# Strassen products of a decoder trunk: a second set of raw weight buffers, another order for each stage's first products, and later sums for two hidden pairs

## The chip, the cores and the metric

The kernel runs on one core of a Trainium2 chip. The metric is the device time of one execution in microseconds (us). Engine names as in the profile: PE (TensorE matmuls), PEld (its weight loads), DVE (VectorE), ACT (ScalarE), POOL (GpSimd), SP (SyncE, which here issues nearly all DMAs).

## The reference

A decoder trunk over 1024 positions with a width of 1024 and two layers, all in float32. Layer 0 mixes tokens with a chunked spatial gate, layer 1 with dilated window attention (three groups of eight heads, head width 64). After each mixer comes a dense MLP:

```python
for layer in range(DEPTH):
    y = _rms_norm(h, mix_norm_g[layer])
    ...
    h = h + y
    y = _rms_norm(h, mlp_norm_g[layer])
    h = h + jnp.square(jax.nn.relu(y @ w_up[layer])) @ w_down[layer]
return _rms_norm(h, final_norm_g)
```

`w_up` is 1024 x 4096 and `w_down` 4096 x 1024, so the two MLPs and the attention's 1024 x 4608 `w_qkv` are most of the work.

## The kernel before, in words

Everything is kept transposed: the stream `h` is eight tiles of 128 rows by 1024 positions. Each float32 operand is split into a high part (rounded by ScalarE, L203) and the rest (a VectorE subtraction, L204), and each block of 128 x 128 by 512 takes three matmuls (`three`, L359).

*Seven products.* The up projection, the down projection and the attention's q, k, v products work on 2 x 2 blocks by a Strassen scheme of seven products instead of eight (`product`, L364): the outputs c11, c12, c21, c22 of a pair of output tiles come from products 1 to 7 and a few sums. A product is 12 matmuls of 512 columns in the up projection, which has 16 pairs q = 0 to 15 in each layer. The order of the products is written out by hand: 5, 6, 1, 7, 3, 2, 4 in `mlp` (L690) and `Down.run` (L819), and 6, 1, 5, 7, 2, 3, 4 in `seven` (L1076, attention). Some products go into the bank of an earlier one, to be added there (3 on 5's, 2 on 1's, 4 on 7's); such a product has to wait until the earlier content is read. There are eight PSUM banks: three of a pool for `mm_bank`, five for `at_bank`.

*Weights.* `Weights` (L370) loads four raw blocks of a pair (`raw`, L161, four buffers in all), forms the combinations on POOL (L389 to L394) and splits each of the seven (tile `wp`; eight buffers). `ahead` does a step of the next pair's weights after each product of this one: 4, then 1, then 5, 6, 7, 3, 2. A raw buffer is free when its split has read it; the next load into it waits for that on SP's queue, and what stands behind on SP waits too.

*Inputs.* `Terms` (L424) makes the input combinations t1 to t7 of a stage while its first output tiles (q = 0 and 1 in the up projection, four tiles in the attention) are computed in the plain, classical way, since these need no combinations. The first half of the positions is s = 0, the second s = 1. After that come the pairs in seven products, from q = 2 on.

*Hidden pairs.* The up projection's outputs go through a squared ReLU on ScalarE (L673, L674). The down projection, whose inner index is the 15 first hidden pairs, needs seven combinations of each (`hidden_terms`, L676: four VectorE sums), which are stored to DRAM and loaded again (`Down.inputs`, L814). The down projection goes through 18 groups t; a full group has four hidden pairs (28 input tiles) and products of 12 matmuls; the first and last groups are smaller.

*Buffers.* `slot` gives one of 38 slots of 4 KB a partition for `h`, the inputs' split pairs and more; `temp` one of 11 of 2 KB (tag t), `spare` one of 2 (tag b).

*Order.* PE's instructions keep the order of the program. On the other engines a scheduler places them when the program is built, by its own estimate of readiness and by the place in the program; `tc.high_priority(offset=PRIO)` moves an instruction up by 60 places. Small side tasks of the attention (scores, transposes, values) are put between the products by `Flow`, which counts PE's time in ns and starts a task when its time has come; `LAT` holds these delays.

Of the kernel before, what the change touches and what calls it, by code (L numbers as in the profile page):

```python
# [10 lines left out]
F32 = mybir.dt.float32  # L11
# [6 lines left out]
P = 128  # L18
# [94 lines left out]
def trunk(ctx: ExitStack, tc: tile.TileContext, xT, w_u, w_v, w_o, w_s, b_s, w_qkv, w_bo, rel,  # L113
# [255 lines left out]

    class Weights:  # L370


        def __init__(self, src, own=None, place=None):
            self.own, self.place = own or raw, place or wpair
            self.w = {}
            self.r = {ij: load(src(*ij), self.own()) for ij in ((1, 0), (1, 1), (0, 0), (0, 1))}
# [7 lines left out]
        def steps(self):  # L384
# [11 lines left out]
            for p, src in ((5, r[1, 0]), (6, r[1, 1]), (7, r3), (3, r[0, 0]), (2, r[0, 1])):  # L396
                self.split(p, src)
                yield

# [289 lines left out]

    def mlp(layer, x, first, last):  # L690


        def up_weights(q):
            return Weights(up(layer, q))
# [4 lines left out]
        for s in range(2):  # L699
# [4 lines left out]
            for b, (q, i) in zip(banks, tiles):  # L704
# [3 lines left out]
                if s and i:  # L708
                    hidden_terms(q, c[q, 0, 0], c[q, 1, 0], c[q, 0, 1], c[q, 1, 1], c[q, 0, 0])
# [6 lines left out]
        for q in range(2, 16):  # L716
# [4 lines left out]
            d = at_bank()  # L721
            product(d, w[5], x.t[5])
            more()
            c22 = temp()
            nc.scalar.activation(c22, d, AF.Copy)  # L725
            if down:
                down.take(14, held, SEVEN[:4])
            b = at_bank()
            product(b, w[6], x.t[6])
            more()  # L730
            if down:
                down.take(14, held, SEVEN[4:])
            a = mm_bank()
            product(a, w[1], x.t[1])
            more()
            u = temp()
            with tc.high_priority(offset=PRIO):
                nc.scalar.activation(u, a, AF.Copy)  # L738
                nc.vector.tensor_tensor(u, u, b, op=ALU.add)
            if down:  # L740
                down.early(SEVEN[:4])
            e = at_bank()
            product(e, w[7], x.t[7])
            more()
            with tc.high_priority(offset=PRIO):
                nc.vector.tensor_tensor(c22, c22, e, op=ALU.add)  # L746
            nc.vector.tensor_tensor(c22, c22, u, op=ALU.add)
            squared(c22)
            if down:
                down.early(SEVEN[4:])  # L750
            product(d, w[3], x.t[3], True)
            more()
            c12 = temp()
# [788 lines left out]
```

## Time and profile before

| what | value |
|---|---|
| runs of the kernel before | 2202.07 us median of 3 (2201.95 to 2205.04) |
| the profiled execution: time | 2201.35 us |
| its span, first to last instruction | 2199.6 us |
| mean granted TensorE clock | 0.987 |
| VectorE busy, share of the span | 1664.0 us, 76% |
| ScalarE busy | 1132.7 us, 51% |
| POOL busy | 608.3 us, 28% |
| mean DMA rate | 110 GB/s |

In the rows of the order of time, the columns are the start in us, the length in us, engine, line, operation, the tile written and the tiles read, shapes, and the number of instructions merged; in brackets stands the idle time of the engine before, and what ended it. `SPq` is SP's queue, where the DMAs are issued.

### The profile page before, as it was taken

How to read it: one execution, taken by the hardware profiler on the slowest of the kernel's cores; microseconds unless marked ns; L12 is line 12 of the kernel's file. 1: busy time of each engine (PE TensorE's matmuls, PEld its weight loads, DVE VectorE, ACT ScalarE, POOL GpSimd, SP SyncE). 2: the span in 40 equal slices, each digit the busy share in tenths (PEclk: the TensorE clock that was granted, in tenths of full speed). 3: DMA queues.
4: the chain of work that ended last, by engine and by line, in shares of the span. 5: the costliest groups of instructions: out<-in, count | busy, mean ns of one | idle time of the engine just before them, and what ended most of it. 6: DMA issues, size and time to landing. Idle time of an engine off the chain costs nothing.

```text
span 2199.6 us, 30242 instructions
## 1 busy us (share of the span) xinstructions
PE 2129.9 (97%) x10242; PEld 1758.3 (80%) x10242; DVE 1664.0 (76%) x2984; ACT 1132.7 (51%) x2294; POOL 608.3 (28%) x442
## 2 busy tenths in 40 slices
PE   7999999999999999998999999999989999999998
PEld 5888886888877888786888788887878888778887
DVE  6875259777788887788787877877887767888866
ACT  6744235555565444346665666664455556544433
POOL 1100114333323332443212222201333332332345
PEclk9999999999999999998999999999999999999999
DMA  6321113444444443321112111141044443554432
GB/s 221 100 83 48 48 41 112 157 151 151 151 163 162 158 157 120 110 82 45 45 42 46 42 53 42 46 161 47 29 168 153 154 148 128 175 166 152 151 110 77
DMA packets 155935, 241.81 MB, mean 110 GB/s; under 512 B 33161, under 2 KB 47620, under 8 KB 155780
## 3 DMA queue, kind: packets, MB, share of 16 engines
q1 hardware_dynamic: 154880, 238.65, 33.3%
q8 instruction: 80, 1.31, 0.3%
q10 hardware_dynamic: 900, 1.23, 0.2%
q14 instruction: 75, 0.61, 0.1%
HBM read 176.21 MB, written 63.61 MB: 109 GB/s over the span
## 4 chain that ended last, share of the span: by engine, by line
PE 76%; DVE 12%; issue 3%; ACT 3%; DMA 3%; POOL 1%; SPq 0%; DVEq 0%; POOLq 0%; ACTq 0%
PE mm L180 37%; PE at L180 37%; DVE wp L204 2%; DVE t L204 2%; PE at L187 2%; DMA r<-in_w_dn 1%; DVE y L204 1%; DMA t<-hid 1%; ACT t L1143 1%; ACT wp L203 1%; DVE h L833 1%; DVE q L1062 1%; DVE k L1062 1%; DVE tr L204 1%; DVE hx L204 1%
## 5 line engine op out<-in xcount | busy, mean ns | idle before, releaser
L203 ACT ACTIVATE wp<-r 128x512 fp32r<-128x512 f32 (+3 forms) x492 | 295.2, 604 | 352.2 <-PE at L180 165.1
L204 DVE TENSOR_TENSOR wp<-r,wp 128x512 fp32r<-128x512 f32 (+3 forms) x492 | 385.5, 787 | 76.2 <-ACT wp L203 73.6
L180 PE MATMUL at<-hx,wp 128*128 128x512 f32 x1770 | 414.4, 390 | 5.5 <-DVE h L833 2.8
L180 PE MATMUL mm<-y,wp 128*128 128x512 f32 x1608 | 404.6, 398 | 1.3 <-ACT t L738 0.8
L180 PEld LDWEIGHTS at<-hx,wp 128*128 128x128 f32 x1770 | 331.9, 188 | 77.0 <-DVE h L833 3.4
L389 POOL TENSOR_TENSOR t<-r 128x512 f32<-128x512 f32 (+3 forms) x78 | 110.3, 1414 | 907.3 <-DMA r<-in_w_up 281.5
L180 PEld LDWEIGHTS mm<-y,wp 128*128 128x128 f32 x1608 | 302.9, 191 | 68.2 <-ACT t L738 1.7
L180 PE MATMUL at<-t,wp 128*128 128x512 f32 x1344 | 318.7, 393 | 8.2 <-DVE t L746 8.2
L180 PEld LDWEIGHTS at<-t,wp 128*128 128x128 f32 x1344 | 255.2, 190 | 62.6 <-DVE t L746 9.0
L180 PE MATMUL mm<-t,wp 128*128 128x512 f32 x768 | 192.5, 397 | 2.3 <-DVE t L204 2.1
L180 PE MATMUL mm<-hx,wp 128*128 128x512 f32 x708 | 172.2, 390 | 5.6 <-DVE b L859 5.6
L261 POOL TENSOR_TENSOR t<-t 128x512 f32<-128x512 f32 (+1 forms) x54 | 69.1, 1279 | 385.4 <-ACT t L252 383.5
L204 DVE TENSOR_TENSOR hx<-t,hx 128x512 fp32r<-128x512 f32 x192 | 164.1, 870 | 11.7 <-ACT hx L203 11.6
L180 PEld LDWEIGHTS mm<-t,wp 128*128 128x128 f32 x768 | 141.5, 189 | 33.0 <-DVE t L204 2.5
L180 PEld LDWEIGHTS mm<-hx,wp 128*128 128x128 f32 x708 | 132.4, 188 | 34.9 <-ACT wp L203 5.0
L180 PE MATMUL mm<-y,whi 128*128 128x512 f32 x512 | 158.3, 390 | 0.0
L203 ACT ACTIVATE hx<-t 128x512 fp32r<-128x512 f32 x192 | 117.9, 627 | 52.5 <-DMA t<-hid 47.8
L180 PE MATMUL at<-y,wp 128*128 128x512 f32 x552 | 138.5, 392 | 3.0 <-ACT t L725 3.0
L833 DVE TENSOR_TENSOR h<-h,at 128x512 f32<-128x512 f32 x144 | 98.1, 683 | 51.6 <-PE at L180 50.5
L394 POOL TENSOR_TENSOR r<-r 128x512 f32<-128x512 f32 (+3 forms) x78 | 106.6, 1366 | 94.2 <-issue 77.3
L391 POOL TENSOR_TENSOR r<-r 128x512 f32<-128x512 f32 (+3 forms) x78 | 118.3, 1516 | 47.4 <-DVE wp L204 43.7
L180 PEld LDWEIGHTS at<-y,wp 128*128 128x128 f32 x552 | 103.7, 189 | 26.6 <-ACT t L725 3.8
(212 smaller groups left out, 3270.8 us busy)
## 6 DMA issues: line engine op xcount, KB each, us to landing
t<-hid SPq DMA_DIRECT2D x182, 256.0 KB, 4.6
hid<-t SPq DMA_DIRECT2D x140, 256.0 KB, 2.3
r<-in_w_up SPq DMA_DIRECT2D x128, 256.0 KB, 2.7
r<-in_w_dn SPq DMA_DIRECT2D x88, 256.0 KB, 2.6
r<-in_w_qkv SPq DMA_DIRECT2D x72, 256.0 KB, 2.7
hid<-b SPq DMA_DIRECT2D x56, 256.0 KB, 2.2
r<-in_w_v SPq DMA_DIRECT2D x48, 256.0 KB, 3.5
h<-in_xT SPq DMA_DIRECT2D x16, 256.0 KB, 4.3
```

Of the source, the lines that this page charges most:

```text
L180: nc.tensor.matmul(out, lhsT, rhs, **kw)
L187: nc.tensor.transpose(out, src, ident)
L203: nc.scalar.activation(hi, src, AF.Copy)
L204: nc.vector.tensor_tensor(lo, src, hi.bitcast(F32), op=ALU.subtract)
L261: nc.gpsimd.tensor_tensor(self.acc, self.acc, sq, op=ALU.add)
L389: tt(r3, r[0, 0], r[1, 0], op=ALU.subtract)
L391: tt(r[1, 1], r[1, 0], r[0, 0], op=ALU.subtract)
L394: tt(r[0, 0], r[0, 1], r[1, 1], op=ALU.subtract)
L833: engine.tensor_tensor(hs[i, s], hs[i, s], src, op=ALU.add)
L1062: nc.vector.scalar_tensor_tensor(lo, a, sc, hi.bitcast(F32), op0=ALU.mult, op1=ALU.subtract)
L1143: nc.scalar.activation(p[:, c], p[:, c], AF.Exp, bias=m, scale=-1.0, accum_out=dn)
```

## The change

1. Weights of the up projection from q = 4 on and of the down projection's groups t = 1 to 16 take only two of their four raw blocks from the four raw buffers; the other two share one slot (`mixed`). So two pairs' raw blocks can be there at once.
2. The first pair in seven products of each up projection (q = 2) and of the attention runs in the order 1, 3, 6, 2, 7, 5, 4, with more banks, and its weights are split in the order 4, 1, 3, 6, 2, 7, 5. The copy of the first product and all sums that read banks are placed 60 places up.
3. The other pairs of the up projection go 6, 1, 5, 7, 2, 3, 4, and the default order of the weights' splits becomes 4, 1, 2, 5, 6, 7, 3 (the down projection's order of products stays).
4. The squares of the classical pairs q = 0 and 1 are stored as they are; their four sums are made at the end of q = 5 and q = 8 from four reloaded tiles (`classical_terms`).
5. The transposes of the first attention unit's values come 5000 ns later in `Flow`.

```diff
+    def mixed():
+        got = []
+        def one():
+            if not got:
+                two = slot((P, 2, HALF), F32, "r2")
+                got.extend([raw(), two[:, 1, :], raw(), two[:, 0, :]])
+            return got.pop()
+        return one
...
-            for p, src in ((5, r[1, 0]), (6, r[1, 1]), (7, r3), (3, r[0, 0]), (2, r[0, 1])):
-                self.split(p, src)
+            src = {2: r[0, 1], 5: r[1, 0], 6: r[1, 1], 7: r3, 3: r[0, 0]}
+            for p in self.late:
+                self.split(p, src[p])
                 yield
+    FIRST = (3, 6, 2, 7, 5)
...
+    def classical_terms(q):
+        c11, c12, c22, c21 = (load(hidden_tile(q, what), temp()) for what in (1, (0, 1), 3, 2))
+        t3, t4 = spare(), spare()
+        tt = nc.vector.tensor_tensor
+        tt(t3, c22, c12, op=ALU.subtract)
+        tt(c12, c12, c11, op=ALU.subtract)
+        tt(c11, c22, c12, op=ALU.subtract)
+        tt(t4, c21, c11, op=ALU.subtract)
+        kept(q, {7: t3, 5: c12, 6: c11, 4: t4})
...
-            return Weights(up(layer, q))
+            return Weights(up(layer, q), own=mixed() if q > 3 else None, **(dict(late=FIRST) if q == 2 else {}))
...
-                if s and i:
-                    hidden_terms(q, c[q, 0, 0], c[q, 1, 0], c[q, 0, 1], c[q, 1, 1], c[q, 0, 0])
+                what = {(0, 0): 1, (1, 0): 2, (0, 1): (0, 1), (1, 1): 3}[i, s]
+                kept(q, {what: c[q, i, s]})
...
+            if q == 2:
+                a = mm_bank()
+                product(a, w[1], x.t[1])
+                more()
+                u = first_sum(a)
+                d = at_bank()
+                product(d, w[3], x.t[3])
+                more()
+                b = at_bank()
+                product(b, w[6], x.t[6])
+                more()
+                plus(u, b, u)
+                product(a, w[2], x.t[2], True)
+                more()
+                c11 = temp()
+                squared(c11, a)
+                e = at_bank()
+                product(e, w[7], x.t[7])
+                more()
+                c22 = plus(u, e)
+                f = at_bank()
+                product(f, w[5], x.t[5])
+                more()
+                plus(c22, f, c22)
+                c12 = plus(u, f)
+                plus(c12, d, c12)
+                squared(c12)
+                squared(c22)
+            else:
...
             product(e, w[4], x.t[4], True)
             more()
+            c21 = plus(u, e)
             squared(c21)
+            if q in (5, 8):
+                classical_terms((q - 5) // 3)
...
-                    wn = self.weights(t + 1, **(dict(own=temp, place=pair) if t == 16 else {}))
+                    wn = self.weights(t + 1, **(dict(own=temp, place=pair) if t == 16 else dict(own=mixed())))
...
-            flow.add(v_side(i, t, part), LAT["ve"] + (500 if b is None else 1500))
+            flow.add(v_side(i, t, part), LAT["ve"] + (500 if b is None else 1500) + (5000 if i == 0 else 0))
...
+        if first:
+            a = one(1)
+            u = copied(a)
+            d = one(3)
+            plus(u, one(6), u)
+            one(2, a)
+            put_out(0, 0, a)
+            e = one(7)
+            c22 = plus(u, e)
+            f = one(5)
+            put_out(1, 1, c22, f, True)
+            put_out(0, 1, plus(u, f), d, True)
+        else:
...
-            w = Weights(qkv(*quads[0]))
+            w = Weights(qkv(*quads[0]), late=FIRST)
```

`first_sum` and `copied` are a ScalarE copy of a bank, `plus` a VectorE sum, all under `tc.high_priority(offset=PRIO)`; `one(p)` in `seven` runs product p in a new `mm_bank`, or adds it to the bank that it is given.

156 lines of the change are left out of this document (78 added, 78 removed).

## Prediction

> **What bounds the kernel now.** I read the page first, then the list of what TensorE waited for, and then the order of time around the longest of those waits.
>
> ```profile
> span 2199.6 us, 30242 instructions
> PE 2129.9 (97%) x10242; PEld 1758.3 (80%) x10242; DVE 1664.0 (76%) x2984; ACT 1132.7 (51%) x2294; POOL 608.3 (28%) x442
> PE at L180 <- DVE t L746: 8.2, 2, 4.1
> PE mm L180 <- DVE b L859: 6.5, 4, 2.2
> PE at L187 <- ACT t L1019: 4.5, 1, 4.5
> PE at L180 <- DVE h L833: 3.5, 4, 1.3
> PE at L180 <- ACT t L725: 3.0, 2, 2.1
> PE at L180 <- ACT hx L203: 2.2, 2, 1.1
> PE mm L180 <- DVE t L204: 2.1, 1, 2.1
> ```
>
> TensorE (PE) is busy for 2129.9 of 2199.6 us, and the change leaves its matmuls as they are. So only the remaining 70 us can be won, and what a slowed TensorE clock costs. The columns of the waits are total us, times, longest. L725, L738 and L746 belong to the first pair of seven products of each up projection (each once a layer; L738 shows below); L859, L833 and hx to the down projection; L1019 and the 2.1 of t L204 to the start of the attention products. Here is that first pair, in layer 0 and then in layer 1 (start, length, instructions, idle time before):
>
> ```profile
> 355.47 5.60 PE L180 MATMUL at<-t,wp 128*128 128x512 f32 x24
> 367.34 3.01 PE L180 MATMUL at<-y,wp 128*128 128x512 f32 x12 [0.83 <-ACT t L725]
> 370.84 3.01 PE L180 MATMUL mm<-y,wp 128*128 128x512 f32 x12 [0.49 <-ACT t L738]
> 377.95 10.03 PE L180 MATMUL at<-t,wp 128*128 128x512 f32 x36 [4.10 <-DVE t L746]
> 387.82 2.88 PE L180 MATMUL mm<-y,wp 128*128 128x512 f32 x12
> 390.54 2.88 PE L180 MATMUL at<-t,wp 128*128 128x512 f32 x12
> ...
> 1591.37 5.60 PE L180 MATMUL at<-t,wp 128*128 128x512 f32 x24
> 1604.62 3.02 PE L180 MATMUL at<-y,wp 128*128 128x512 f32 x12 [2.12 <-ACT t L725]
> 1615.10 11.20 PE L180 MATMUL at<-t,wp 128*128 128x512 f32 x36 [4.11 <-DVE t L746]
> 1626.14 2.88 PE L180 MATMUL mm<-y,wp 128*128 128x512 f32 x12
> ```
>
> A product is 12 matmuls and takes 390.54 - 387.82 = 2.72 us. The row at 387.82 is product 1 of the next pair (q = 3), nine products after 355.47. Without waits it would start at 355.47 + 9 x 2.72 = 379.95, so layer 0 loses 7.87 us here. Layer 1 should reach it at 1591.37 + 24.48 = 1615.85 and does at 1626.14: 10.29 lost. The idle times do not add up to that, because the clock fell after the long wait (us, PE busy, granted clock, DMA share, GB/s):
>
> ```profile
> 378.00:382.00 4.00, 4.00 (x11) 0.57 0.52 178
> 1614.00:1621.00 7.00, 5.90 (x14) 0.51 0.60 200
> 420.00:439.10 19.10, 19.10 (x86) 15.82 (x85) 13.47 (x17) 10.09 (x17) 6.30 (x5) 1.00 0.46 152
> ```
>
> The 36 matmuls from 377.95 took 387.82 - 377.95 = 9.87 us where three products take 8.16: 1.71 us of clock. The last row is a later pair, with the busy time of PE, PEld, DVE, ACT and POOL: PE has no idle time there, so nothing that speeds a later pair's weights can gain in it.
>
> **The change, part by part.** *First pair, order 1, 3, 6, 2, 7, 5, 4.* Before, product 3 accumulated on product 5's bank, product 2 on product 1's and product 4 on product 7's, and each waited for a read (L725, L738, L746). Now 3, 6, 7 and 5 have banks of their own and only 2 and 4 wait. Product 2 needs ScalarE's copy of product 1. That copy is now raised by 60 places, but so are the squares of the classical tiles, which come earlier in the program, and ScalarE was late:
>
> ```profile
> 363.78 1.16 ACT L674 ACTIVATE t<-t 128x512 f32<-128x512 f32 x2
> ...
> 366.71 0.58 ACT L725 ACTIVATE t<-at 128x512 f32<-128x512 f32 x1
> ...
> 1601.37 1.16 ACT L674 ACTIVATE t<-t 128x512 f32<-128x512 f32 x2
> 1602.41 0.64 ACT L203 ACTIVATE t<-t 128x512 fp32r<-128x512 f32 x1
> 1603.97 0.60 ACT L725 ACTIVATE t<-at 128x512 f32<-128x512 f32 x1
> ```
>
> These are the last squares of each layer, and L725 in each. Right behind them the copy (0.58) ends at 363.78 + 1.16 + 0.58 = 365.5 and at 1603.1. Product 2 is fourth, due at 355.47 + 8.16 = 363.63 and at 1591.37 + 8.16 = 1599.53. So it waits 1.9 and 3.6 us. Bounds: nothing if the copy goes ahead of the squares; 366.71 + 0.58 - 363.63 = 3.7 and 1603.97 + 0.60 - 1599.53 = 5.0 if it stays where L725 stood. I take the middle, as the program's priorities put it there. An idle time of 3.6 us lies between waits of 2.22 (a row below; the 12 matmuls after it took 3.00, full speed) and 4.10 (half clock after it); it is nearer to the second, so I add 1.7 for the clock in layer 1.
>
> [...]
>
> *Product 4.* L746 read the bank late because VectorE (DVE) was behind with sums and splits:
>
> ```profile
> 1603.87 1.76 DVE L204 TENSOR_TENSOR t<-t,t 128x512 fp32r<-128x512 f32 x1
> 1607.25 0.68 DVE L679 TENSOR_TENSOR b<-t 128x512 f32<-128x512 f32 x1
> 1607.85 1.78 DVE L204 TENSOR_TENSOR wp<-r,wp 128x512 fp32r<-128x512 f32 x1
> 370.33 1.60 POOL L391 TENSOR_TENSOR r<-r 128x512 f32<-128x512 f32 x1 [0.69 <-DVE wp L204]
> 1607.47 1.61 POOL L391 TENSOR_TENSOR r<-r 128x512 f32<-128x512 f32 x1 [0.69 <-DVE wp L204]
> ```
>
> The eight sums of the two classical pairs (L679 to L685, 8 x 0.68 = 5.4 us) leave this place. Product 7's bank is now read by one sum, and product 5 (2.72 us) runs in between. I count this wait as gone: 0.
>
> *What is late next* is the second pair, which now begins with product 6. Its weights are ready after POOL's L391, a ScalarE copy (0.64) and a VectorE split (at worst 1.78, beside POOL): 370.33 + 1.60 + 2.42 = 374.4 and 1607.47 + 1.61 + 2.42 = 1611.5. Product 6 is due four products after product 2 has started: 365.5 + 10.88 = 376.4 and 1614.0. The wait of product 2 covers it by 2.0 and 2.5 us. Without that wait product 6 would be due at 374.5 and at 1591.37 + 7 x 2.72 = 1610.4 and would itself wait 1.1 in layer 1.
>
> So the two starts give 7.87 - 1.9 = 6.0 and 10.29 - 3.6 - 1.7 = 5.0: **11.0 us**, with bounds of 6.1 (rival 1) and 17 (7.87 + 10.29 - 1.1).
>
> *The sums made later*, at q = 5 and 8: four loads on SP's queue, four sums and four stores each. VectorE has 13.47 + 4 x 0.68 = 16.2 of 19.10 us to do, so PE hides it: 0. Bare, it would be 2.7 us at each of four places, 11 in all. The loads stand on SP ahead of the weights of q = 7 and 10; the second raw set has those a pair ahead.
>
> *Steady pairs in order 6, 1, 5, 7, 2, 3, 4*: one ScalarE copy less (10.09 of 19.10 busy), each bank is reused two products after it filled, as products 1 and 7's were; 0.
>
> *Second raw set.* In the up projection 0, as said. In the down projection SP is held by it (rows: total, times, longest; then SP's and PE's order of time):
>
> ```profile
> SPq L169 <- DVE wp L204: 192.5, 60, 7.8
> 677.70 7.95 SPq L169 DMA_DIRECT2D r<-in_w_dn  x3
> 685.70 3.27 SPq L169 DMA_DIRECT2D t<-hid  x7
> 697.13 3.00 PE L180 MATMUL mm<-hx,wp 128*128 128x512 f32 x12 [2.22 <-DVE b L859]
> ```
>
> Between 630 and 900 us, SP waits 192.5 us for a weight split to free a raw buffer, and the loads of the hidden inputs queue behind: seven of them from 685.70, right after weights that took 7.95. Their splits then hold VectorE up, and PE waits 2.22 at 697.13. I count one such wait per layer as gone: 2 x 2.2 = **4.4 us**. Bounds: 0, and all of L859, L833 and hx, 6.5 + 3.5 + 2.2 = 12.2.
>
> *Attention's first products* take banks from the pool of three only:
>
> ```profile
> 996.75 2.82 PE L180 MATMUL mm<-t,wp 128*128 128x512 f32 x10
> 1006.97 1.11 PE L187 MATMUL at<-ident,t 128*128 128x128 f32 x4 [4.53 <-ACT t L1019]
> 1005.81 1.11 ACT L1019 ACTIVATE t<-mm 128x512 f32<-128x512 f32 x1
> 1010.29 1.11 DVE L1062 SCALAR_TENSOR_TENSOR q<-mm,q 128x512 fp32r<-128x512 f32 x1
> ```
>
> Two of the three hold classical tiles until L1019 (1006.92) and L1062 (1011.40). Before, product 6 ran and then the transposes waited for L1019. Now product 1 runs, the transposes come later, and product 3 waits for the same L1019, for a bank. At 1006.92 twelve matmuls are done in either case: 0. Bounds: a gain of 2.1 + 4.5 = 6.6 if ScalarE's order changes; a loss of 1011.40 - 1006.92 - 2.72 = 1.8, product 6 waiting for the third bank.
>
> **Sum.** The profiled execution took 2201.35 us (its span is 2199.6); the median of the runs before is 2202.07, 0.03% above. 2201.35 - 11.0 - 4.4 = **2185.9 us**. A measurement of this kernel can tell about 0.2%, 4.4 us, from no change.
>
> **Rivals.** *1. The waits only change owner.* The copy stays where L725 was: layer 0 gains 7.87 - 3.7 - 1.7 = 2.5, layer 1 10.29 - 5.0 - 1.7 = 3.6, attention loses 1.8, the down projection gains nothing: 2201.35 - 4.3 = 2197.0. For it: ScalarE takes its queue in order, and that order was late by a slow VectorE. Against it: the copy's new priority. Chance 0.14, no change.
>
> *2. The second pair takes the wait.* Its splits go 4, 1, 2, 5, 6, so four stand ahead of 6 on VectorE; if all five take 1.78 beside POOL and four sums of 0.68 come between, 11.6 us from 1603.87 (where the classical sums ended and a split of 1.76 began) plus that 1.76 end at 1617.2, against 1614.0 due: 3.2 late, and much the same in layer 0, 6.4 in all: 2192.3. For it: the 1.78 row against 0.68. Against: four slow splits need four POOL sums beside them. Chance 0.14, faster.
>
> [...]
>
> *3. Slots run out, slower.* A raw set now takes a slot of 38. In the down projection 8 hold the stream and 28 the four groups' inputs, so the two that were free for the next inputs hold raw weights. Splits of the inputs then wait for a product to end, their loads keep the temporaries, and SP is blocked again. At 2.2 us (the wait at 697.13) in half of the 20 full groups that is 22 us: 2201.35 - 11.0 + 22 = 2212. It decides from 11.0 / 2.2 = 5 groups on. Against it: an input's slot is freed seven products before its successor is used. Chance 0.12.
>
> *4. Everything gives.* 17 at the starts, 12.2 in the down projection, 6.6 at the attention: 2165.5; half of the surplus, 2176. For it: the waits are real; against it: the banks and ScalarE's order. Chance 0.12.
>
> **How the numbers follow.** The forecast has 0.48, with a range of its own of 2179 to 2192. Faster: 0.48 + 0.14 + 0.12 = 0.74; within 0.2%: 0.14; slower: 0.12. The range 2172 to 2199 leaves out rival 3 and the far end of rival 4.
>
> **What would show it.** Right: no wait for L746's successor; one wait of 2 and one of 3 to 4 us before the fourth product of the first pairs, on the copy of product 1; SP waiting far less than 192.5 us on weight splits; the attention's first gap unchanged in size, now ahead of product 3. Wrong: idle PE in later pairs at q = 5 to 9, or new short waits on hx in every group of the down projection.

## The result, and the profile after

The changed kernel takes 2182.13 us (median of five runs, 2178.83 to 2192.09) against 2204.02 (median of five, 2201.95 to 2207.61): ratio 0.9907, 95% interval 0.9881 to 0.9933, faster by 0.9%. The forecast was 2185.9, range 2172 to 2199. The profiled execution has the time of the median, 2182.13, and its span is 19.2 us shorter than before.

The page of the changed kernel, and its list of what TensorE waited for (total us, times, longest):

```profile
span 2180.4 us, 30158 instructions
...
PE 2121.8 (97%) x10242; PEld 1755.2 (80%) x10242; DVE 1647.1 (76%) x2987; ACT 1126.3 (52%) x2266; POOL 600.9 (28%) x442
```

```profile
PE mm L180 <- ACT t L750: 6.6, 2, 4.3
...
PE mm L180 <- ACT t L1079: 5.6, 1, 5.6
...
PE at L180 <- DVE h L893: 1.6, 2, 0.8
...
PE mm L180 <- DVE b L919: 0.4, 1, 0.4
```

The wait for a VectorE sum ahead of product 4 (8.2 us in all before) is gone from the list; the copy of product 1 (L750) stands in its place with 6.6. L919 and L893, the successors of the down projection's L859 and L833, went from 6.5 and 3.5 to 0.4 and 1.6.

The first pair of both layers in TensorE's order of time:

```profile
357.28 4.24 PE L180 MATMUL mm<-y,wp 128*128 128x512 f32 x18
...
369.31 4.22 PE L180 MATMUL mm<-y,wp 128*128 128x512 f32 x12 [2.35 <-ACT t L750]
373.34 11.59 PE L180 MATMUL at<-t,wp 128*128 128x512 f32 x48
384.76 2.88 PE L180 MATMUL mm<-y,wp 128*128 128x512 f32 x12
...
1579.01 4.24 PE L180 MATMUL mm<-y,wp 128*128 128x512 f32 x18
...
1592.97 4.51 PE L180 MATMUL mm<-y,wp 128*128 128x512 f32 x12 [4.28 <-ACT t L750]
1597.32 11.04 PE L180 MATMUL at<-t,wp 128*128 128x512 f32 x48
1608.20 2.88 PE L180 MATMUL mm<-y,wp 128*128 128x512 f32 x12
```

The 18 matmuls at 357.28 are 6 classical ones (1.36 us) and product 1, so the pair begins at 358.64, and at 1580.37 in layer 1. Product 1 of the next pair, now eight products later, would start at 358.64 + 8 x 2.72 = 380.40 and at 1602.13. It starts at 384.76 and 1608.20: 4.36 and 6.07 us lost, where 7.87 and 10.29 were lost before. The one wait of each layer is where the prediction put it, before the fourth product, and behind it the clock is low (granted 0.69 and 0.63; 4.22 and 4.51 us for 12 matmuls).

Where the 19.2 us come from is best read from the traces by stage. TensorE's 10242 matmuls stand in every kernel in the same stages, so the time between the starts of two numbered matmuls can be compared (us, difference to the profiled execution of before; the first column is its own length). The kernels are those of the experiments below.

| stage | before | changed | order alone | sums alone | raw set alone | sums and raw set | changed, no raw set |
|---|---|---|---|---|---|---|---|
| start to the first pair, layer 0 | 349.95 | +2.90 | +1.22 | +4.65 | +1.84 | +0.89 | +3.60 |
| first pair, layer 0 | 32.35 | -3.51 | -0.09 | -5.08 | +0.03 | -5.05 | -3.57 |
| rest of the up projection | 242.08 | 0.00 | 0.00 | 0.00 | 0.00 | 0.00 | 0.00 |
| first groups of the down projection | 78.68 | -2.94 | -0.30 | -0.35 | -1.54 | -1.37 | -1.32 |
| its middle | 191.53 | 0.00 | 0.00 | 0.00 | 0.00 | 0.00 | 0.00 |
| its end, attention's classical tiles | 96.63 | -4.64 | +0.11 | -1.57 | -4.57 | -4.59 | -2.15 |
| attention | 500.38 | -3.08 | -1.23 | -0.70 | -1.64 | -2.45 | -3.97 |
| first pair, layer 1 | 34.77 | -4.22 | -2.94 | -5.85 | -0.45 | -5.81 | -4.29 |
| first groups of the down projection, layer 1 | 78.63 | -3.23 | -0.26 | +0.12 | -0.70 | -0.59 | -1.42 |

Left out are the stretch between the attention and layer 1's first pair (0.00 in the changed kernel) and the rest of layer 1 (0.7 us shorter in it, all at its end).

The stages that were full of matmuls agree to 0.01 us; others differ for kernels with the same code there. The start differs by 0.9 to 4.6 us, most of it in the first 80 matmuls, which no edit touches. Among all kernels here with the changed kernel's code in a stage, the first pair differs by 0.3 us in layer 0 and 1.2 in layer 1, the down projection's first groups gain between 1.5 and 3.3 us, and the attention lies between 4.2 us shorter and 0.5 longer than before. The single time of a kernel therefore says little: the changed kernel's own five runs lie 13 us apart. The experiments below are read by stage, and a difference within these bounds can be chance.

### The profile page after: what moved, and what is told of

Read it like the earlier page. It is cut to its first block, busy times and chain, and to the rows that moved or that the text cites. A ratio compares the mean times of both kernels' runs of the same rounds, so it can differ in the third digit from the quotient of the medians.

```text
span 2180.4 us, 30158 instructions
## 1 busy us (share of the span) xinstructions
PE 2121.8 (97%) x10242; PEld 1755.2 (80%) x10242; DVE 1647.1 (76%) x2987; ACT 1126.3 (52%) x2266; POOL 600.9 (28%) x442
## 3 DMA queue, kind: packets, MB, share of 16 engines
q8 instruction: 80, 1.31, 0.2%
q10 hardware_dynamic: 900, 1.23, 0.2%
## 4 chain that ended last, share of the span: by engine, by line
PE 82%; DVE 9%; ACT 3%; issue 2%; DMA 2%; POOL 0%; SPq 0%; DVEq 0%; ACTq 0%; POOLq 0%
PE at L180 41%; PE mm L180 39%; PE at L187 2%; DVE wp L204 2%; DVE t L204 1%; ACT t L1219 1%; ACT wp L203 1%; DVE k L1122 1%; DMA t<-hid 1%; DVE tr L204 0%; DMA r<-in_w_v 0%; DVE h L332 0%; DVE q L1122 0%; DVE h L893 0%; DMA h<-hd 0%
## 5 line engine op out<-in xcount | busy, mean ns | idle before, releaser
L204 DVE TENSOR_TENSOR wp<-r,wp 128x512 fp32r<-128x512 f32 (+3 forms) x492 | 380.9, 778 | 40.1 <-ACT wp L203 36.3
L180 PE MATMUL at<-t,wp 128*128 128x512 f32 x1344 | 314.3, 389 | 0.0
L204 DVE TENSOR_TENSOR hx<-t,hx 128x512 fp32r<-128x512 f32 x192 | 179.8, 948 | 5.7 <-ACT hx L203 5.6
L893 DVE TENSOR_TENSOR h<-h,at 128x512 f32<-128x512 f32 x144 | 97.5, 679 | 55.4 <-PE at L180 55.3
L756 DVE TENSOR_TENSOR t<-t,at 128x512 f32<-128x512 f32 x116 | 79.0, 683 | 74.9 <-PE at L180 74.7
```

Of the source, the lines that this page charges most:

```text
L180: nc.tensor.matmul(out, lhsT, rhs, **kw)
L204: nc.vector.tensor_tensor(lo, src, hi.bitcast(F32), op=ALU.subtract)
L756: nc.vector.tensor_tensor(out, x, y, op=ALU.add)
L893: engine.tensor_tensor(hs[i, s], hs[i, s], src, op=ALU.add)
```

## The experiments

A pair "loses" what TensorE's next pair is late by, worked out as above. Before: 7.87 and 10.29, 18.2 in all. Changed: 4.36 and 6.07, 10.4 in all.

**The first pair's order alone**, put into the kernel before (2200.24 us):

```diff
-            return Weights(up(layer, q))
+            return Weights(up(layer, q), **(dict(late=FIRST) if q == 2 else {}))
...
+            if q == 2:
...
+                product(a, w[1], x.t[1])
...
+                product(d, w[3], x.t[3])
...
+                product(b, w[6], x.t[6])
```

> The kernel before with the first pair's order 1, 3, 6, 2, 7, 5, 4 alone (q = 2 of both up projections: banks, raised copy and sums, split order); classical sums at the start, one raw set, attention as before. Measure: what the two starts lose against waiting nowhere (before 7.9 + 10.3 = 18.2 us; changed kernel 4.4 + 6.1 = 10.5). Theory A (order and later sums are both needed: product 2 waits for ScalarE's copy in any case, and with the eight sums of 0.68 still on VectorE the sum that reads product 7's bank is up to 5 us later, so product 4 waits again): 15 to 19 us lost. Theory B (the order alone does it): 10 to 11.5 lost. Theory C (the later sums alone do it): about 18 lost.

The first pairs lose 7.8 and 7.35, 15.1 in all, as theory A has it. TensorE waits for the copy of product 1 and then for VectorE ahead of product 4:

```profile
367.10 3.01 PE L180 MATMUL mm<-y,wp 128*128 128x512 f32 x12 [1.84 <-ACT t L727]
...
379.31 5.97 PE L180 MATMUL at<-t,wp 128*128 128x512 f32 x18 [3.75 <-DVE t L733]
```

With the classical sums still in place, the order gains nothing in layer 0, where the wait for VectorE stays, and 2.9 us in layer 1, where it is down to 1.67.

**The later classical sums alone**, in the kernel before (2193.1 us):

```diff
-                if s and i:
-                    hidden_terms(q, c[q, 0, 0], c[q, 1, 0], c[q, 0, 1], c[q, 1, 1], c[q, 0, 0])
+                what = {(0, 0): 1, (1, 0): 2, (0, 1): (0, 1), (1, 1): 3}[i, s]
+                kept(q, {what: c[q, i, s]})
...
+            if q in (5, 8):
+                classical_terms((q - 5) // 3)
```

> The kernel before with only the classical pairs' sums made later (at q = 5 and 8). Theory A: the waits on the copies stay (0.8 + 0.5 and 2.1 + 0.3) and the wait of product 4 shrinks from 4.1 to 1 or 2 us, so the starts lose 8 to 13 us of the 18.2. Theory B (the order alone does it): 17 to 18 lost. Theory C (the later sums alone do it): 10 to 11.5, the same as the changed kernel. In all three, no idle PE at q = 5 to 9.

The first pairs lose 2.8 and 4.4, 7.2 in all. That is less than in the whole change, and less than any of the three theories had. The sums alone are enough for the gain at the starts; the whole change gives 3.2 us of it back.

**The second raw set alone**, in the kernel before (2192.04 us):

```diff
-            return Weights(up(layer, q))
+            return Weights(up(layer, q), own=mixed() if q > 3 else None)
...
-                    wn = self.weights(t + 1, **(dict(own=temp, place=pair) if t == 16 else {}))
+                    wn = self.weights(t + 1, **(dict(own=temp, place=pair) if t == 16 else dict(own=mixed())))
```

> The kernel before with only the second raw set (up projection from q = 4, down projection). Theory A (SP's queue was held by the raw buffers): the down projection's first groups, from the end of the last up pair to the first full stretch without idle time, become 2.9 and 3.2 us shorter in the two layers, as in the changed kernel; the two starts of the up projection lose 18.2 us as before; total 2193 to 2196. Theory B (the changed split order or the earlier start did it): the down projection gains under 1 us, total 2200 to 2203. SP's waits on weight splits between 630 and 900 us fall from 192 us to under 130 by A.

Nothing is gained at the first pairs (17.7 lost), 1.5 and 0.7 us at the down projection's first groups, well short of theory A's 2.9 and 3.2, and 4.6 at its end in layer 0. SP's waits on weight splits between 630 and 900 us fall to 165.2, not under 130. The gain at the end is three waits of before, 3.1 us, of which one is left in the changed kernel (before, then changed), and the clock behind them (before):

```profile
915.74 1.63 PE L180 MATMUL mm<-hx,wp 128*128 128x512 f32 x6 [1.41 <-DVE b L859]
...
922.15 0.94 PE L180 MATMUL at<-hx,y 128*128 128x512 f32 x3 [0.71 <-DVE h L833]
...
924.06 1.12 PE L180 MATMUL mm<-hx,y 128*128 128x512 f32 x3 [0.97 <-DVE b L859]
```

```profile
917.73 0.96 PE L180 MATMUL mm<-hx,y 128*128 128x512 f32 x3 [0.36 <-DVE b L919]
```

```profile
924.62:928.03 3.41, 3.41 (x10) 2.65 (x9) 1.86 (x3) 0.00 (x0) 3.25 (x3) 0.50 0.18 62
```

In that stretch TensorE (the second number) is busy throughout at a granted clock of 0.50 (the number before the last two), so half of it, 1.7 us, is lost. That part doesn't need the raw set: the kernel with the later sums alone has the same three waits without the slow clock behind them, and gains its 1.6 us at this place by that.

At the first groups the wait at 697.13 goes, and of before also these two:

```profile
647.01 0.50 PE L180 MATMUL at<-hx,wp 128*128 128x512 f32 x1 [1.12 <-ACT hx L203]
...
678.29 8.45 PE L180 MATMUL at<-hx,wp 128*128 128x512 f32 x36 [1.20 <-DVE h L833]
```

But new ones appear there, in the changed kernel these:

```profile
636.43 2.58 PE L180 MATMUL at<-hx,wp 128*128 128x512 f32 x10 [1.20 <-DVE wp L204]
...
658.87 7.82 PE L180 MATMUL at<-hx,wp 128*128 128x512 f32 x33 [0.82 <-DVE h L893]
```

**The changed kernel with the attention's part undone** (2182.54 us):

```diff
-            flow.add(v_side(i, t, part), LAT["ve"] + (500 if b is None else 1500) + (5000 if i == 0 else 0))
+            flow.add(v_side(i, t, part), LAT["ve"] + (500 if b is None else 1500))
...
-            w = Weights(qkv(*quads[0]), late=FIRST)
+            w = Weights(qkv(*quads[0]))
...
-        seven(w, xa, more, lambda i, *x: out(two[i], *x), None if wn else lambda: flow.add(ahead_of_last()), n == 0)
+        seven(w, xa, more, lambda i, *x: out(two[i], *x), None if wn else lambda: flow.add(ahead_of_last()))
```

> The changed kernel with the attention part taken back (products in the order 6, 1, 5, 7, 2, 3, 4 from the first pair on, default split order, transposes not put off). Theory A (the first gap waits for the evacuation of the classical banks in either order): the attention stage from its first pair to its end is within 2 us of the changed kernel's, total 2179 to 2184. Theory B (the new order there is what shortened the stage by 3 us): 2 to 5 us longer, total 2182 to 2187.

From the end of the down projection to the end of the attention it gains 7.03 us on before, the changed kernel 7.72. That is within theory A's 2 us, and the difference of 0.7 is far below what the attention differs by with the same code, so the part shows no effect of its own. The gaps at the attention's first products, first in the changed kernel, then with the part undone:

```profile
997.35 4.21 PE L180 MATMUL mm<-y,wp 128*128 128x512 f32 x9 [5.65 <-ACT t L1079]
```

```profile
995.34 1.22 PE L180 MATMUL mm<-t,wp 128*128 128x512 f32 x2 [6.41 <-ACT wp L203]
999.37 4.04 PE L180 MATMUL mm<-t,wp 128*128 128x512 f32 x10 [2.81 <-DVE wp L204]
```

The undone form keeps the new default order of splits, in which product 6, its first, is split fifth, so it isn't quite the attention of before (gaps of 2.15 and 4.53).

**The squares behind the copy.** In the changed kernel, ScalarE's squares of four classical tiles stand ahead of the copy:

```profile
367.62 1.16 ACT L689 ACTIVATE t<-t 128x512 f32<-128x512 f32 x2
368.65 0.61 ACT L750 ACTIVATE t<-mm 128x512 f32<-128x512 f32 x1
...
1591.27 1.16 ACT L689 ACTIVATE t<-t 128x512 f32<-128x512 f32 x2
1592.31 0.61 ACT L750 ACTIVATE t<-mm 128x512 f32<-128x512 f32 x1
```

Here they are put behind it (2181.42 us):

```diff
                 with tc.high_priority(offset=PRIO):
-                    squared(c[q, i, s], b)
+                    if s:
+                        nc.scalar.activation(c[q, i, s], b, AF.Relu)
+                        continue
+                    squared(c[q, i, s], b)
...
+                ins = nc.cur_bb.bb.instructions[-1]
+                with tc.issue_after(ins):
+                    for z, i in tiles:
+                        nc.scalar.activation(c[z, i, 1], c[z, i, 1], AF.Square)
```

> The changed kernel, with one thing moved: the four squares of the classical tiles that ScalarE makes just ahead of the copy of product 1 are issued behind that copy, and their stores with them. In the changed kernel the waits before product 2 (the fourth of the first pair) are 2.35 us in layer 0 and 4.28 in layer 1, and nine products lose 4.36 and 6.07 us. Theory A (the copy is late because ScalarE takes its queue in order and two squares of 1.16 us stand ahead of it): the two waits shrink by up to 2 x 1.16 to about 0.1 and 2.0, layer 0 keeps the full clock, so the starts lose about 1 and 3 us instead of 10.4 in all, and the time is about 2176 (from 2182.1). Theory B (another wait is right behind): product 4 or the second pair waits for VectorE's sums instead, the starts still lose over 8.4 of 10.4, and the time stays within 2180 to 2184.

Both theories have a share. The two waits on the copy fall by 1.0 each, to 1.35 and 3.25, so ScalarE's order of issue does hold the copy. But in layer 0 a second wait appears ahead of product 4:

```profile
370.28 3.02 PE L180 MATMUL mm<-y,wp 128*128 128x512 f32 x12 [1.35 <-ACT t L768]
...
380.41 5.75 PE L180 MATMUL at<-t,wp 128*128 128x512 f32 x24 [1.68 <-DVE t L759]
```

The pairs lose 3.64 and 5.15, 8.8 in all, 1.6 less than changed; that loss and the time are in theory B's ranges.

**Product 2 two places later** (order 1, 3, 6, 7, 5, 2, 4; 2186.51 us):

```diff
-                product(a, w[2], x.t[2], True)
-                more()
-                c11 = temp()
-                squared(c11, a)
                 e = at_bank()
...
                 plus(c22, f, c22)
+                product(a, w[2], x.t[2], True)
+                more()
+                c11 = temp()
+                squared(c11, a)
```

> The changed kernel with the first pair's products in the order 1, 3, 6, 7, 5, 2, 4: product 2 comes sixth instead of fourth, so it is due 2 x 2.72 = 5.4 us later, behind the copy of product 1 that was 2.35 and 4.28 us late. Theory A (only the copy of product 1 is late): the wait on the copy is gone in both layers, the starts lose less than 3 us in all instead of 10.4, time about 2175. Theory B (VectorE is as late as ScalarE): product 4, now right behind product 2, waits for VectorE's sums, which in the changed kernel were made at 375 to 378 us, up to 4 us a layer; the starts lose 7 to 11, time 2179 to 2183.

The copy isn't waited for any more, and product 4 waits for VectorE instead, as theory B has it, in layer 0:

```profile
377.04 7.35 PE L180 MATMUL at<-t,wp 128*128 128x512 f32 x24 [2.88 <-DVE t L756]
```

In layer 1 it waits 3.48. The pairs lose 4.8 and 7.3, 12.1 in all, and the time is 2186.51, both even more than theory B expected.

**The first pair in the order of before**, all else changed (2183.7 us):

```diff
-            return Weights(up(layer, q), own=mixed() if q > 3 else None, **(dict(late=FIRST) if q == 2 else {}))
+            return Weights(up(layer, q), own=mixed() if q > 3 else None, **(dict(late=(5, 6, 7, 3, 2)) if q == 2 else {}))
...
+                product(d, w[5], x.t[5])
+                more()
+                c22 = first_sum(d)
...
+                product(b, w[6], x.t[6])
...
+                product(a, w[1], x.t[1])
```

> The changed kernel with the first pair's products in the order of before (5, 6, 1, 7, 3, 2, 4), the raised copies and sums, the second raw set and the later classical sums all kept. With the later sums alone, that order lost about 7.2 us in the two starts; the changed kernel loses 10.4. Theory A (the new order costs: it needs the first copy earlier than ScalarE has it): the starts lose 5 to 8 us and the time is 2177 to 2180. Theory B (the 3.2 between those two kernels is chance, or comes from the raised priorities): the starts lose 9.5 to 11.5 and the time is 2181 to 2184.

The pairs lose 4.6 and 6.3, 10.9: theory B. The order of the first pair's products alone is not what costs the 3.2.

**The sums and the second raw set, with every order of before** (2181.92 us), the edits of both single parts put into the kernel before:

```diff
+            return Weights(up(layer, q), own=mixed() if q > 3 else None)
...
+                kept(q, {what: c[q, i, s]})
...
+            if q in (5, 8):
+                classical_terms((q - 5) // 3)
...
+                    wn = self.weights(t + 1, **(dict(own=temp, place=pair) if t == 16 else dict(own=mixed())))
```

> The kernel before with the later classical sums and the second raw set, and with every order of before: first pair, steady pairs, weight splits and attention. Theory A (the new orders cost at the starts of the up projection, where the sums alone lost 7.2 us against 10.4 in the changed kernel, and earn at the starts of the down projection, where the raw set alone gained 1.5 and 0.7 against 2.9 and 3.2): the two add to about nothing, 3.2 better and 4.0 worse, and the time is 2181 to 2185 against 2182.1. Theory B (the new orders are needed for the gain): over 2188. Theory C (they only cost): below 2180.

Theory A. The pairs lose 2.8 and 4.5, 7.3 in all, the down projection's first groups gain 1.4 and 0.6, and the time is that of the whole change. Product 4 in layer 0, here and in the kernel with the old first order:

```profile
368.95 3.03 PE L180 MATMUL at<-y,wp 128*128 128x512 f32 x12 [1.31 <-ACT t L748]
372.50 3.03 PE L180 MATMUL mm<-y,wp 128*128 128x512 f32 x12 [0.52 <-ACT t L761]
375.56 8.50 PE L180 MATMUL at<-t,wp 128*128 128x512 f32 x36
```

```profile
377.27 7.32 PE L180 MATMUL at<-t,wp 128*128 128x512 f32 x24 [2.71 <-DVE t L756]
```

The first pair begins at 356.60 here and at 358.08 there, so product 4 starts 18.96 and 19.19 us after it, nearly the same. But here the lateness comes in pieces of 1.31 and 0.52 and what follows runs at full speed (8.50 for 36, 2.83 a product), and there in one piece of 2.71 with 24 matmuls in 7.32, 1.72 more than the 5.60 of a full clock. In layer 1 the same 24 matmuls took 7.38, 1.78 more: together 3.5 of the 3.6 us between 7.3 and 10.9. In the kernel with the old first order the raised copies leave no wait ahead of products 3 and 2 in layer 0, and the whole lateness comes before product 4; but the two kernels also differ in the later pairs' order and in the order of their splits, and no run separates these.

**The changed kernel without the second raw set** (2187.89 us):

```diff
-            return Weights(up(layer, q), own=mixed() if q > 3 else None, **(dict(late=FIRST) if q == 2 else {}))
+            return Weights(up(layer, q), **(dict(late=FIRST) if q == 2 else {}))
...
-                    wn = self.weights(t + 1, **(dict(own=temp, place=pair) if t == 16 else dict(own=mixed())))
+                    wn = self.weights(t + 1, **(dict(own=temp, place=pair) if t == 16 else {}))
```

> The changed kernel without the second raw set; the first pair's order and the later classical sums stay. Theory A (the raw set's gain is at the start of the down projection and at its end, and does not hang on the rest): the down projection gets its waits back, about 2.9 and 3.2 us at its two starts and 3 to 4.6 at its end in layer 0, the starts of the up projection stay within 1 us of 10.4 lost, and the time is 2190 to 2194 against 2182.1. Theory B (the later sums free enough of VectorE that the raw set is no longer needed): less than 4 us is given back, 2182 to 2186.

Between the two theories: 1.6 and 1.8 us are given back at the first groups and 2.5 at the end of layer 0's, 5.9 in all. The first groups' part is no more than that stage differs by with the same code. The starts lose 10.3, as theory A expected.

**The down projection's splits in the order of before** (2185.14 us):

```diff
-            wn = down.weights(0) if down else up_weights(q + 1)
+            wn = down.weights(0, late=(5, 6, 7, 3, 2)) if down else up_weights(q + 1)
...
-                    wn = self.weights(t + 1, **(dict(own=temp, place=pair) if t == 16 else dict(own=mixed())))
+                    wn = self.weights(t + 1, **(dict(own=temp, place=pair) if t == 16 else dict(own=mixed(), late=(5, 6, 7, 3, 2))))
```

> The changed kernel, with the weight splits of the down projection in the order of before (5, 6, 7, 3, 2 instead of 2, 5, 6, 7, 3; product 4's and 1's stay first). Theory A (splitting product 2's weights first frees their raw buffer earlier, and that is why the changed kernel gains 2.9 and 3.2 us at the starts of the down projection where the second raw set alone gained 1.5 and 0.7): the starts of the down projection lose 1.3 to 2.5 us each again, and the time is 2184.5 to 2187. Theory B (the later gain there comes from the lighter VectorE or the order of the last pair of the up projection): those two stages stay within 0.5 us, time 2181 to 2183.

The two stages gain 3.2 and 2.8 where the changed kernel gains 2.9 and 3.2, so theory B: the order of the splits isn't what makes them better than with the raw set alone. The time lies above theory B's range, mainly since the attention, whose code is the same, took 2.9 us longer than in the changed kernel. This run tells something else. Its first pair has the code of the changed kernel, and the same wait of 2.35, but the full clock after it (granted 1.00 up to 373.34, where the changed kernel had 0.69):

```profile
369.15 3.04 PE L180 MATMUL mm<-y,wp 128*128 128x512 f32 x12 [2.35 <-ACT t L750]
...
379.10 5.76 PE L180 MATMUL at<-t,wp 128*128 128x512 f32 x24 [1.47 <-DVE t L756]
```

A new wait of 1.47 stands ahead of product 4, and the pair loses 4.45, as the changed kernel's 4.36. In the changed kernel product 4 ran from about 384.76 - 2 x 2.72 = 379.32 on, right behind the VectorE sum that it needs, the last line here:

```profile
371.06 4.06 DVE L204 TENSOR_TENSOR wp<-r,wp 128x512 fp32r<-128x512 f32 x3
375.04 0.67 DVE L756 TENSOR_TENSOR t<-t,at 128x512 f32<-128x512 f32 x1
375.64 2.89 DVE L204 TENSOR_TENSOR wp<-r,wp 128x512 fp32r<-128x512 f32 x2
378.45 0.67 DVE L756 TENSOR_TENSOR t<-t,at 128x512 f32<-128x512 f32 x1
```

So what the half clock cost in layer 0 would have been waited for anyway: in its order of issue here, VectorE sets the end of the first pair, with five weight splits (7 us) ahead of and between its sums.

**The splits behind the sum**: the kernel with the squares behind the copy, and VectorE's first splits of the next pair's weights behind the sum of products 1 and 6 (2188.7 us):

```diff
-            more()
+            if q != 2:
+                more()
...
                 plus(u, b, u)
+                ins = nc.cur_bb.bb.instructions[-1]
+                with tc.issue_after(ins):
+                    for _ in range(4):
+                        more()
```

> The kernel with the four squares behind the copy of product 1, and one thing more: in the first pair VectorE's splits of the next pair's weights (4, 1, 2 and 5) are issued behind the sum of products 1 and 6, not ahead of it. In that kernel this sum came at 376.3 and 1596.4 us, 15.7 and 17.0 us after product 1 had started, behind splits that wait for GpSimd in order; product 4 then waited 1.68 us in layer 0 for the sum after it, and the starts lost 3.64 and 5.15 us. Theory A (VectorE's order of issue makes the sums late): the sum comes about 5 us earlier, product 4 waits for nothing, layer 0 loses about 1.5 to 2 instead of 3.64, layer 1 is left with its 3.25 on the copy and the clock after it (about 4.8 to 5.2): the starts lose 6 to 7 in all, and the time is 2178 to 2181. Theory B (the splits are needed as early as they stand): product 6 of the second pair waits instead, for its weight split, 1 to 3 us in each layer, and the starts lose 8 to 11, 2181 to 2184.

The sum came at 370.70 where it had come at 376.29, and layer 0 loses 2.54 instead of 3.64, layer 1 5.26: 7.8 in all, between theory A's 6 to 7 and theory B's 8 to 11, with 0.58 left ahead of product 4. Moving the splits does make the sum earlier, by 5.6 us. The time missed theory A's range: stages whose code is the same as in the changed kernel were longer, the start by 2.6, the down projection's first groups by 2.9 and the attention by 3.6.

**The first reads behind the copy too** (2186.41 us, median of six; ratio to before 0.9936, interval 0.9917 to 0.9954); the lines are against the kernel just above:

```diff
-                        nc.scalar.activation(c[q, i, s], b, AF.Relu)
                         continue
...
-                    for z, i in tiles:
-                        nc.scalar.activation(c[z, i, 1], c[z, i, 1], AF.Square)
+                    for bank, (z, i) in zip(banks, tiles):
+                        squared(c[z, i, 1], bank)
```

> The kernel with the four squares behind the copy of product 1 and VectorE's splits behind the sum, and one thing more: ScalarE's four first reads (the relus, about 0.5 us each) of those classical tiles go behind that copy too, so it comes up to 2.1 us earlier. There the copy was waited for 1.37 us in layer 0 and 3.24 in layer 1 (half clock after it), and the starts lost 2.54 and 5.26 us. Theory A (ScalarE's queue holds the copy, nothing else is close): no wait in layer 0 and about 1.2 in layer 1 at full clock, the starts lose 1 to 2 and 1.2 to 2.5, 2 to 4.5 in all against 10.4 in the changed kernel; over five rounds 4 to 8 us below the changed kernel, 2174 to 2179. Theory B (VectorE's sum of products 1 and 7 or the second pair's first weights are right behind): product 4 or 6 waits as long as the copy no longer does, the starts lose over 6, and the time is within 0.2% of the changed kernel's 2182.1.

Theory B, and more. The copy's waits are down to 0.16 and 2.04, and product 4 waits for VectorE (both layers):

```profile
369.49 3.01 PE L180 MATMUL mm<-y,wp 128*128 128x512 f32 x12 [0.16 <-ACT t L767]
...
381.42 5.74 PE L180 MATMUL at<-t,wp 128*128 128x512 f32 x24 [3.49 <-DVE t L759]
...
1592.80 3.06 PE L180 MATMUL mm<-y,wp 128*128 128x512 f32 x12 [2.04 <-ACT t L767]
...
1604.68 7.36 PE L180 MATMUL at<-t,wp 128*128 128x512 f32 x24 [3.39 <-DVE t L759]
```

The pairs lose 4.2 and 7.7, 11.9 in all. VectorE's splits wait for GpSimd, whose first weight sum now starts after 10.09 us of idle time on ScalarE's square, 12.9 us into the pair; in the changed kernel it started 10.7 into it (this kernel, then the kernel with the squares behind the copy):

```profile
373.88 1.29 POOL L401 TENSOR_TENSOR t<-r 128x512 f32<-128x512 f32 x1 [10.09 <-ACT t L689]
```

```profile
371.45 1.30 POOL L401 TENSOR_TENSOR t<-r 128x512 f32<-128x512 f32 x1 [8.07 <-DMA r<-in_w_up]
```

That sum writes a temporary; there are eleven, and the classical tiles hold eight until they are squared and stored. That this makes the sum late was not tried by itself. The second row shows what else holds it: the load of a raw block of the next pair, q = 3. In the changed kernel that load is issued at 366.63, when a split of q = 2 has freed a raw buffer, and lands at 369.13, just before the sum starts at 369.29. The second raw set begins with q = 4, so it doesn't help here; giving it to q = 3 was not tried either. No kernel here is measurably faster than the changed one.

## Why the prediction was right, point by point

The time came out 3.8 us below the forecast, and part of that closeness is luck: the starts of the up projection gave 3.3 us less than forecast and the down projection 6.4 more, and two differences that the forecast did not have, in stages that differ by as much with the same code, cancelled (the start 2.9 longer, the attention 3.1 shorter).

*The starts of the up projection: 11.0 forecast, 7.7 measured* (3.5 and 4.2). The mechanism was right for the waits: the wait of product 4 (L746) is gone, and the copy of product 1 is waited for before the fourth product, with 2.35 and 4.28 us against 1.9 and 3.6. Both were larger because the copy ended 10.6 and 12.55 us after the pair's start (369.26 and 1592.92), where the rows of before gave 10.05 and 11.7. The clock of 1.7 was put into layer 1 alone; here it came in both, but in layer 0 of the kernel with the old splits, which has the same first pair, it did not (12 matmuls in 3.04 us), and product 4 waited 1.47 instead. Of product 4 the text said "I count this wait as gone: 0". That was too much: its sum ended at 379.12 (1602.38 in layer 1), and product 4 started at about 379.3 (1602.8), so with VectorE's order of issue as it is, product 4 could hardly have started earlier, whatever the copy does. Taking the copy's wait away gained nothing: with product 2 two places later the copy isn't waited for, and the pairs lose 4.8 and 7.3.

*Which edit gains there.* The prediction gave the order and the sums one common term. The sums alone gain 10.9 us of the 18.2; the order alone 3.0; the whole change 7.7. The eight classical sums (5.4 us of VectorE) are the gain, since VectorE's queue is the bound. In the whole change the lateness comes in one wait (2.35 and 4.28) with a low clock behind it; with the sums alone it comes in two or three short ones (0.17 to 2.10) without (12 matmuls in 3.00 to 3.06). The first pair's order by itself isn't the reason (10.9 lost with the old one); between the raised copies and the other new orders no run separates. With the sums and the raw set but every order of before, the time is 2181.92, so the orders and priorities show no gain of their own.

*The 1.7 of clock in layer 1* was put there because 3.6 us lies nearer to the 4.10 than to the 2.22, and layer 1 paid. The length of a wait alone doesn't tell this here: behind waits of 2.35 and 2.71 the clock was low too (12 matmuls in 4.22, 24 in 7.32), and behind one of 3.49 it wasn't (24 in 5.74).

*The down projection: 4.4 forecast, 10.8 measured* (2.9, 3.2 and 4.6). "I count one such wait per layer as gone" was the mis-sized term. Those two waits went, and more, at the end of layer 0's above all: the list's L859 fell by 6.1 us, within the bound of 12.2. About 1.7 of the 10.8 is clock at that end, which the sum did not have. The part of the raw set is 5.9 us by its absence; by itself it gains 6.8, of which 1.6 to 1.7 is that clock. What more the first groups gain in the changed kernel (2.9 and 3.2 against 1.4 and 0.6 with the sums and the raw set) stays open. The order of the splits is not it, and some of it can be chance: in the kernel with the splits behind the sum, whose code is the same there, they gain only 1.5 and 1.8.

*SP waiting far less* was wrong, though TensorE's waits fell. Between 630 and 900 us of the changed kernel:

```profile
SPq L169 <- DVE wp L204: 156.4, 42, 11.1
SPq L169 <- PE at L180: 28.7, 10, 3.3
```

192.5 us became 156.4, in fewer and longer waits. SP still stands still; it does so with another pair's raw blocks already loaded. The second row is new: loads that wait for a product to free a slot, rival 3's mechanism, which took nothing from the middle of the stage (0.00).

*Attention: 0 forecast, nothing measurable* for its own part. The gap of 5.65 stands ahead of product 3 on the same ScalarE read (L1079, before L1019), as said, where before there were gaps of 2.15 and 4.53. The attention's 3.1 us are within what that stage differs by between kernels with the same attention.

*The later pairs and the sums made later: 0*, and 0.00 in every kernel.

*The rivals.* Rival 1, that the waits only change owner, had 2.5 + 3.6 = 6.1 us for the starts, nearer to the 7.7 than the forecast's 11.0; its 3.7 and 5.0 for the copy were not reached, and it was wrong in giving the down projection nothing. Rival 2's wait of product 6 of the second pair never came in the changed kernel. The slow splits that it counted did (about 1.4 us each beside GpSimd's sums, where the sums that read a bank took 0.67), but they held product 4's sum. Rival 4's surplus came from the down projection, not from the starts.

## What to carry to other kernels

When a wait of TensorE is taken away, look up when the next wait's releaser ends, on its own engine and in its own order of issue, and count the gain only up to there; here the sum after it was late by as much. Work that can be done elsewhere and stands in the queue of the late engine (eight sums, 5.4 us) was worth more here than any order of the products. And compare stages that begin and end at the same matmul: single times of this kernel differ by more than the edits are worth.

## What the runs showed of the hardware

The clock after a wait of TensorE is not settled by its length. After 2.35 us the next 12 matmuls ran at a mean granted clock of 0.69 in the changed kernel (4.22 us) and at 1.00 in the kernel with the old splits (3.04 us). After 3.49 us the last kernel kept full clock in layer 0 (5.74 for 24 matmuls), and after 3.39 it had not in layer 1 (7.36, at 0.76).

In the traces of before and of the changed kernel the granted clock is 1.00 or 0.50. It changes 21 and 19 times, each time at a multiple of 3.41 us from the first change (to within 0.02 us), and where these points fall differs between the two: 378.49 in layer 0's first pair before, 370.83 in the changed kernel. Below are the stretch of 3.41 us up to 370.83, which holds most of the wait of 2.35, and the one behind it, in the changed kernel; then two of that length at the same wait in the kernel with the old splits; last, two that share the 3.49 of the last kernel. TensorE's busy time is the second number, the clock the one before the last two.

```profile
367.42:370.83 3.41, 1.51 (x7) 1.25 (x8) 1.40 (x2) 3.40 (x7) 1.47 (x2) 1.00 0.80 212
370.83:374.24 3.41, 3.41 (x10) 2.63 (x9) 3.41 (x4) 1.26 (x2) 2.71 (x2) 0.50 1.05 346
```

```profile
367.35:370.76 3.41, 1.61 (x7) 1.35 (x8) 1.40 (x2) 3.31 (x7) 1.48 (x2) 1.00 0.64 218
370.76:374.17 3.41, 3.41 (x17) 2.81 (x16) 3.41 (x4) 1.26 (x2) 2.72 (x2) 1.00 0.96 330
```

```profile
376.33:379.74 3.41, 1.61 (x8) 0.99 (x6) 3.11 (x3) 1.76 (x4) 3.25 (x3) 1.00 0.13 50
379.74:383.15 3.41, 1.73 (x8) 1.43 (x9) 3.41 (x5) 1.72 (x4) 2.31 (x3) 1.00 0.54 148
```

TensorE is idle for 1.90 us (3.41 - 1.51) of the first stretch in the changed kernel, and the next one runs at half clock; it is idle for 1.80 and 1.68 in the others, and the clock stays. In the first pairs of before and of the changed kernel, stretches with 1.90, 2.87, 3.12 and all of 3.41 us idle had half clock behind them, and those with 1.2 and 1.4 full clock. That gives no limit: at the end of layer 0's down projection before, half clock came behind a stretch with 1.67 idle (921.21 to 924.62), and ahead of layer 1's first pair in the changed kernel behind one with no idle time at all (1538.19 to 1541.60). What sets the clock is not shown. A stretch at half clock that is full of matmuls, as from 370.83 above, loses 3.41 / 2 = 1.7 us, the 1.7 of the prediction.

So waits of 2.35 to 3.49 us had half clock behind them in some traces and not in others, and two kernels with the same first pair, the changed one and the one with the old splits, differ by that in layer 0.
